# Half of the second load moved to ScalarE's ring, beside the first load

## The chip, the cores and the metric

One core of a Trainium2 chip. The metric is the device time of one execution in microseconds (us). Runs of one kernel mostly agree within 0.3%.

## The reference

A rotary embedding in float32: `x` of 16 x 512 x 1024 is cut into 16 heads of 64; each head's halves `x1`, `x2` are turned with `cos` and `sin` of 512 x 32.

```python
x1, x2 = x[..., :half_dim], x[..., half_dim:]
rotated = np.concatenate([x1 * cos - x2 * sin, x1 * sin + x2 * cos], axis=-1)
```

33.55 MB are read and as much is written.

## The kernel before

`x` is handled in 8 slabs of 2 batches: 128 partitions of 32 KB, 4.194 MB each. Five slabs fit at a time, so load 5 waits until store 0 has landed. Loads go through SyncE's ring (q1 in the profile), stores through ScalarE's ring (q10), the tables through GpSimd. Loads 1 to 4 are held until `cos` has landed.

```python
def load(s):
    slab[s] = slabs.tile([P, W], f32, tag="slab", name="slab")
    return nc.sync.dma_start(out=slab[s], in_=dram(x, s))

load(0)
# ... cos and sin are loaded through gpsimd
for s in range(1, slots):                 # slots = 5
    tc.add_manual_dep(load(s).ins, table[0].ins.name, ...)   # after cos
# ... tables, and passes: slabs 0, 6 and 7 in two halves, the others whole
cast(passes[0])                           # ScalarE: f32 slab -> bf16 xb
for i, (s, r, n) in enumerate(passes):
    if i + 1 < len(passes):
        cast(passes[i + 1])
    # ... VectorE: two products and a sum in bf16
    nc.scalar.copy(out=xs, in_=xu)        # ScalarE: bf16 -> f32, into the slab
    if r + n == rpp:
        nc.scalar.dma_start(out=dram(out_flat, s), in_=slab[s])
        if s + slots < nslabs:
            load(s + slots)
```

Of the kernel before, what the change touches and what calls it, by code (L numbers as in the profile page):

```python
# [2 lines left out]

# [4 lines left out]


@with_exitstack  # L10
def kernel(
    ctx: ExitStack,
    tc: tile.TileContext,
    x: bass.AP,
    cos: bass.AP,
    sin: bass.AP,
    num_heads: int,
    out: bass.AP,
):
    nc = tc.nc  # L20
    P = nc.NUM_PARTITIONS

    batch, seq, dim = x.shape
    nh = num_heads
    hd = dim // nh
    half = hd // 2
    bf16 = mybir.dt.bfloat16
    f32 = mybir.dt.float32

    nb = 2  # L30
    slots = 5
    nslabs = batch // nb
    rpp = nb * seq // P
    W = rpp * dim
    SP = seq // rpp
    TW = rpp * half

    out_flat = out.rearrange("b s h d -> b s (h d)")

    singles = ctx.enter_context(tc.tile_pool(name="singles", bufs=1))  # L40
    slabs = ctx.enter_context(tc.tile_pool(name="slabs", bufs=slots))
    xpool = ctx.enter_context(tc.tile_pool(name="xpool", bufs=2))
    psum = ctx.enter_context(tc.tile_pool(
        name="psum", bufs=1, space=bass.MemoryType.PSUM))


    def dram(t, s, a=0, n=W):
        return bass.AP(tensor=t.tensor, offset=t.offset + s * nb * seq * dim + a,
                       ap=[[W, P], [1, n]])


    def view(t, offset, *dims):
        return dataclasses.replace(t, offset=t.offset + offset,
                                   ap=[t.ap[0], *[list(d) for d in dims]])


    slab = {}


    def load(s):  # L60
        slab[s] = slabs.tile([P, W], f32, tag="slab", name="slab")
        return nc.sync.dma_start(out=slab[s], in_=dram(x, s))  # L62


    load(0)


    TR = seq // P
    G = rpp // TR
    table = {}  # L70
    raw = singles.tile([P, 2 * TR * half], f32, tag="raw")
    for i, src in enumerate((cos, sin)):
        table[i] = nc.gpsimd.dma_start(out=view(raw, i * TR * half, (1, TR * half)), in_=bass.AP(  # L73
            tensor=src.tensor, offset=src.offset,
            ap=[[TR * half, P], [1, TR * half]]))



    for s in range(1, slots):
        tc.add_manual_dep(  # L80
            load(s).ins, table[0].ins.name,
            mybir.DependencyInfo(mybir.DependencyClass.Sync,
                                 mybir.DependencyReason.DATA),
            reason="issue")



    pick = singles.tile([P, 2 * G * P], bf16, tag="pick")
    nc.gpsimd.memset(pick, 0.0)  # L89
    for g in range(2 * G):  # L90
        part = view(pick, g * P, (SP, P // SP), (1, SP))
        nc.gpsimd.affine_select(  # L92
            out=part, in_=part, compare_op=mybir.AluOpType.not_equal,
            fill=1.0 if g < G else -1.0, base=-(g % G),
            pattern=[[0, P // SP], [-G, SP]], channel_multiplier=1)

    tab1 = singles.tile([P, 2 * TR * half], bf16, tag="tab1")
    nc.gpsimd.tensor_copy(out=tab1, in_=raw)  # L98

    acc = psum.tile([P, 2 * rpp * hd], f32, tag="acc")  # L100
    for i in range(2):
        for h in range(2):
            for g in range(G):
                nc.tensor.matmul(  # L104
                    view(acc, (i * rpp + g * TR) * hd + h * half, (hd, TR), (1, half)),
                    view(pick, (i * h * G + g) * P, (1, P)),
                    view(tab1, i * TR * half, (half, TR), (1, half)),
                    start=True, stop=True)
    tab = singles.tile([P, 2 * rpp * hd], bf16, tag="tab")
    nc.vector.tensor_copy(out=tab, in_=acc)  # L110

    xb = {}


    def cast(u):
        s, r, n = u
        if r == 0:
            xb[s] = xpool.tile([P, W], bf16, tag="xb", name="xb")
        nc.scalar.copy(out=view(xb[s], r * dim, (1, n * dim)),  # L119
                       in_=view(slab[s], r * dim, (1, n * dim)))  # L120




    passes = []
    for s in range(nslabs):
        n = rpp if 1 <= s < nslabs - 2 else rpp // 2
        passes += [(s, r, n) for r in range(0, rpp, n)]


    cast(passes[0])
# [3 lines that stand above are left out]
        xs = view(slab[s], r * dim, (1, n * dim))  # L135
        xu = view(xb[s], r * dim, (1, n * dim))

        t2 = view(slab[s].bitcast(bf16), 2 * r * dim, (1, n * dim))
        for t, a in ((t2, rpp * hd), (xu, 0)):
            nc.vector.tensor_mul(  # L140
                out=t, in0=xu,
                in1=view(tab, a + r * hd, (hd, n), (0, nh), (1, hd)))
        nc.vector.tensor_add(  # L143
            out=xu, in0=xu, in1=view(t2, half, (hd, n * nh), (-half, 2), (1, half)))

        nc.scalar.copy(out=xs, in_=xu)  # L146
# [6 lines that stand above are left out]
# [1 line left out]
_INS = ['x', 'cos', 'sin', 'num_heads']  # L154
_OUTS = [((16, 512, 16, 64), 'float32')]

_NUMBERS = {'num_heads': 16}


# [26 lines left out]
```

## Time and profile before

| | before |
|---|---|
| median, 3 runs | 162.07 us (161.98 to 162.12) |
| VectorE, ScalarE busy | 68%, 71% |
| DMA rate over the span | 419 GB/s |
| slab 0 / slab 1 landed | 13.3 / 23.0 us |
| first store issued | 37.11 us |
| load 5 issued | 61.59 us |
| last store issued; until it landed | 145.28 us; 14.2 us |

The lines behind this stand in the prediction. They are read in this order: who is full, at what rate, where one stage hands over to the next, and how long the last transfer waits in its queue.

### The profile page before, as it was taken

To read this page: it belongs to the slowest core of one execution; us is meant where nothing else is said; L and a number is where in the kernel's file an instruction comes from. 1 tells how busy PE (TensorE), PEld (TensorE's weight loads), DVE (VectorE), ACT (ScalarE), POOL (GpSimd) and SP (SyncE) were. 2 spreads that over 40 slices of the span, in tenths; PEclk is the share of its full clock that TensorE was granted. 3 is DMA by queue.
4 is the path that set the end of the run, shared out by engine and by line. 5 is a ranking of instruction groups with operands and counts; after the bars stand their busy time and mean duration, and the time that the engine had idled before them with its cause. 6 is when DMAs were issued, how large, how long until landed. Compare 5 with 4: busy or idle time off the path is not lost.

```text
span 160.4 us, 169 instructions
## 1 busy us (share of the span) xinstructions
PE 1.0 (1%) x8; PEld 0.8 (1%) x8; DVE 108.5 (68%) x34; ACT 113.5 (71%) x23; POOL 3.4 (2%) x12
## 2 busy tenths in 40 slices
PE   0011000000000000000000000000000000000000
PEld 0010000000000000000000000000000000000000
DVE  0003799999989979997996099939749599930000
ACT  3006939998998999899907997099995999462000
POOL 7000000000000000000000000000000000000000
DMA  7999999999999999999999999999999999999995
GB/s 245 425 409 409 474 425 400 466 441 392 384 400 400 507 400 400 466 441 392 441 474 392 433 482 392 425 482 400 400 507 400 400 474 433 392 449 466 392 433 221
DMA packets 2368, 67.24 MB, mean 419 GB/s; under 512 B 288, under 2 KB 288, under 8 KB 320
## 3 DMA queue, kind: packets, MB, share of 16 engines
q1 hardware_dynamic: 1152, 33.55, 49.5%
q10 hardware_dynamic: 1152, 33.55, 48.4%
q0 software_dynamic: 64, 0.13, 0.2%
HBM read 33.69 MB, written 33.55 MB: 419 GB/s over the span
## 4 chain that ended last, share of the span: by engine, by line
DMA 59%; ACT 17%; issue 9%; DVE 4%; SPq 0%; ACTq 0%; POOLq 0%
DMA slab<-in_x_dram 39%; DMA out_dram<-slab 15%; ACT slab L146 11%; ACT xb L119 6%; DMA raw<-in_cos_dram 4%; DVE xb L140 1%; DVE xb L143 1%; DVE slab L140 1%; SPq L62 0%; ACTq L146 0%; POOLq L167 0%
## 5 line engine op out<-in xcount | busy, mean ns | idle before, releaser
L119 ACT CAST xb<-slab 128x4096 bf16<-128x4096 f32 (+1 forms) x11 | 56.6, 5155 | 27.5 <-DMA slab<-in_x_dram 26.2
L146 ACT CAST slab<-xb 128x4096 f32<-128x4096 bf16 (+1 forms) x11 | 56.6, 5153 | 3.5 <-DVE xb L143 3.5
L140 DVE TENSOR_TENSOR slab<-xb,tab 128x4096 bf16<-128x4096 bf16 (+1 forms) x11 | 35.9, 3260 | 19.9 <-ACT xb L119 19.8
L140 DVE TENSOR_TENSOR xb<-xb,tab 128x4096 bf16<-128x4096 bf16 (+1 forms) x11 | 35.9, 3261 | 0.3
L143 DVE TENSOR_TENSOR xb<-xb,slab 128x4096 bf16<-128x4096 bf16 (+1 forms) x11 | 35.9, 3261 | 0.3
L110 DVE CAST tab<-acc 128x1024 bf16<-128x1024 f32 x1 | 1.2, 1225 | 12.5 <-PE acc L104 12.5
L119 ACT ACT_TABLE_LOAD x1 | 1.3, 1283 | 0.7 <-PEq L167 0.7
L104 PE MATMUL acc<-tab,pick 128*128 128x128 bf16 x8 | 1.0, 305 | 11.5 <-POOL tab L98 11.5
L92 POOL TENSOR_SCALAR_AFFINE_SELECT pick<-pick 128x128 bf16<-128x128 bf16 x4 | 1.0, 288 | 0.1
L104 PEld LDWEIGHTS <-pick 128*128 128x128 bf16 x8 | 0.8, 136 | 11.4 <-issue 8.0
L73 POOL DMA_DIRECT2D raw<-in_cos_dram x1 | 0.7, 674 | 0.8 <-POOLq L167 0.8
L89 POOL MEMSET pick<- 128x512 bf16 x1 | 0.5, 543 | 0.0
L98 POOL CAST tab<-raw 128x256 bf16<-128x256 f32 x1 | 0.4, 396 | 6.9 <-DMA raw<-in_sin_dram 6.9
L73 POOL DMA_DIRECT2D raw<-in_sin_dram x1 | 0.5, 534 | 0.0
L167 POOL MEMSET const-float32-0.0<- 128x1 f32 x1 | 0.1, 99 | 0.2 <-issue 0.2
L167 POOL MEMSET const-bfloat16-1.0<- 128x1 bf16 x1 | 0.1, 102 | 0.0
L167 POOL MEMSET const-uint8-127<- 128x1 uint8 x1 | 0.1, 102 | 0.0
L167 POOL MEMSET const-float32-1.0<- 128x1 f32 x1 | 0.1, 99 | 0.0
## 6 DMA issues: line engine op xcount, KB each, us to landing
slab<-in_x_dram SPq DMA_DIRECT2D x8, 4096.0 KB, 24.5
out_dram<-slab ACTq DMA_DIRECT2D x8, 4096.0 KB, 26.6
raw<-in_cos_dram POOLq DMA_DIRECT2D x1, 64.0 KB, 7.0
raw<-in_sin_dram POOLq DMA_DIRECT2D x1, 64.0 KB, 9.0
```

Of the source, the lines that this page charges most:

```text
L73: table[i] = nc.gpsimd.dma_start(out=view(raw, i * TR * half, (1, TR * half)), in_=bass.AP(tensor=src.tensor, offset=src.offset, ap=[[TR * ...
L89: nc.gpsimd.memset(pick, 0.0)
L92: nc.gpsimd.affine_select(out=part, in_=part, compare_op=mybir.AluOpType.not_equal, fill=1.0 if g < G else -1.0, base=-(g % G), pattern=[[ ...
L98: nc.gpsimd.tensor_copy(out=tab1, in_=raw)
L104: nc.tensor.matmul(view(acc, (i * rpp + g * TR) * hd + h * half, (hd, TR), (1, half)), view(pick, (i * h * G + g) * P, (1, P)), view(tab1, ...
L110: nc.vector.tensor_copy(out=tab, in_=acc)
L119: nc.scalar.copy(out=view(xb[s], r * dim, (1, n * dim)), in_=view(slab[s], r * dim, (1, n * dim)))
L140: nc.vector.tensor_mul(out=t, in0=xu, in1=view(tab, a + r * hd, (hd, n), (0, nh), (1, hd)))
L143: nc.vector.tensor_add(out=xu, in0=xu, in1=view(t2, half, (hd, n * nh), (-half, 2), (1, half)))
L146: nc.scalar.copy(out=xs, in_=xu)
L167: nc = _bacc.Bacc("TRN2", target_bir_lowering=False, num_devices=1)
```

## The change

The intent is to use ScalarE's ring, which has nothing to do for the first 37 us, for a part of slab 1.

```diff
+    early = W // 2
...
     def load(s):
+        if s == 1:
+            return nc.sync.dma_start(out=view(slab[s], early, (1, W - early)),
+                                     in_=dram(x, s, early, W - early))
         slab[s] = slabs.tile([P, W], f32, tag="slab", name="slab")
         return nc.sync.dma_start(out=slab[s], in_=dram(x, s))
     load(0)
+    slab[1] = slabs.tile([P, W], f32, tag="slab", name="slab")
+    nc.scalar.dma_start(out=view(slab[1], 0, (1, early)), in_=dram(x, 1, 0, early))
```

## The prediction

> **What bounds the kernel now.** I read the page's totals first, then the two rings' bytes, the chain of waits, and last each stretch in which one stage hands over to the next. The totals (share of the span; then the mean DMA rate):
>
> ```profile
> PE 1.0 (1%) x8; PEld 0.8 (1%) x8; DVE 108.5 (68%) x34; ACT 113.5 (71%) x23; POOL 3.4 (2%) x12
> DMA  7999999999999999999999999999999999999995
> DMA packets 2368, 67.24 MB, mean 419 GB/s; under 512 B 288, under 2 KB 288, under 8 KB 320
> q1 hardware_dynamic: 1152, 33.55, 49.5%
> q10 hardware_dynamic: 1152, 33.55, 48.4%
> ```
>
> The two compute engines are 68% and 71% busy; the DMA engines are at nine tenths or more in 38 of 40 slices, and the two rings (q1 is SyncE's, with the loads; q10 ScalarE's, with the stores) add up to 98% of the span. So the DMA engines are the bound, and only their first and last slices have idle time. The table by stretch says how fast they go when full (columns: stretch, its length, busy time of the five engines, clock, DMA share, GB/s):
>
> ```profile
> 2.00:4.00 2.00, 0.00 (x0) 0.10 (x1) 0.00 (x0) 0.02 (x1) 1.93 (x6) 1.00 0.83 328
> 4.00:13.00 9.00, 1.01 (x8) 0.74 (x7) 0.49 (x1) 0.00 (x0) 0.47 (x2) 1.00 1.00 430
> 13.00:37.00 24.00, 0.00 (x0) 0.00 (x0) 20.67 (x9) 21.06 (x5) 0.00 (x0) 1.00 1.00 429
> 66.00:122.00 56.00, 0.00 (x0) 0.00 (x0) 42.99 (x13) 45.29 (x8) 0.00 (x0) 1.00 1.00 431
> ```
>
> The decisive row is 4 to 13 us: there the SyncE ring holds slab 0 alone for half of the time and already moves 430 GB/s, as much as both rings together do at 66 to 122 us (431). One ring fills the engines. A slab is 4.194 MB, so it costs 4.194 MB / 431 GB/s = 9.73 us of all the engines, in whichever ring it is.
>
> The timeline and the list of issues give the hand-overs (start, length, instruction, idle time before it; in the issue row, size and us from issue to landing):
>
> ```profile
> 0.74 9.34 SPq L62 DMA_DIRECT2D slab<-in_x_dram  x5
> 13.33 7.11 ACT L119 CAST xb<-slab 128x4096 bf16<-128x4096 f32 x2 [11.31 <-DMA slab<-in_x_dram]
> 23.05 7.02 ACT L119 CAST xb<-slab 128x8192 bf16<-128x8192 f32 x1 [2.61 <-DMA slab<-in_x_dram]
> 29.98 7.11 ACT L146 CAST slab<-xb 128x4096 f32<-128x4096 bf16 x2
> 37.11 0.38 ACTq L148 DMA_DIRECT2D out_dram<-slab  x1
> ...
> 145.28 0.34 ACTq L148 DMA_DIRECT2D out_dram<-slab  x1
> ...
> out_dram<-slab ACTq DMA_DIRECT2D x1, 4096.0 KB, 14.2
> ```
>
> Slab 0 lands at 13.3 us, slab 1 at 23.0, the first store is issued at 37.1, and the last store is issued at 145.28 and needs 14.2 us, to 159.5, which is the end. The chain of waits names loads (39% of the span), stores (15%) and ScalarE's casts (17%), but it follows one dependency at a time; with engines that are full throughout, a shorter link in it gains nothing unless the end moves.
>
> **What the Trainium skill says.** "DMA: Bandwidth & Descriptors", section "Issuing engines are not separate DMA queues": transfers of all issuers run on the same 16 engines and interleave, and issuing from several saves only issue time. The trace agrees: 430 GB/s with one ring, 431 with two; an issue costs 0.34 to 0.47 us. The same page, "Queues, rings and completion order": each engine takes turns between the rings that have work, by packets. The trace agrees: between 45 and 51.5 us q1 moved 1.47 MB and q10 1.54 MB. The same page, "Where 436 GB/s comes from", puts the ceiling at 435 GB/s; the 431 here is 1% below it, so no higher rate is to be expected.
>
> **The change, part by part.** Removed: nothing; bytes stay 67.24 MB. Added: one issue on ScalarE at the start (about 0.4 us, while it waits 11.3 us for slab 0 anyway), 128 rows of 16 KB where 128 rows of 32 KB become 256 of 16 KB, and a second landing for slab 1's cast to wait for. None is on the path.
>
> Moved: 2.10 MB now compete with slab 0 from the first microsecond. Slab 0 has 4.19 MB in 32 KB rows, the half slab the same number of rows of 16 KB; taking turns, both end together after 6.29 MB. So **slab 0 lands later by 2.10 MB / 431 GB/s = 4.9 us**, at 13.3 + 4.9 = 18.2. Slab 1 is complete when the same 8.39 MB have moved as before: 23.0. The second half of slab 1 and slabs 2 to 4 still wait for cos to land, at 8.3 us before and perhaps 10 with three queues taking turns; the SyncE ring holds slab 0 until about 18, so nothing starves. The tables (sin landed at 11.0, product ready at 13.7) come some 3 us later, still before the first cast ends at 18.2 + 3.6 = 21.8.
>
> ScalarE, if the order of its work stays: the two half casts 18.2 to 25.3, slab 1's cast (7.0) to 32.3 without the wait of 2.61 us that it has now, the two copies (7.1) to 39.5. VectorE starts at 21.8 instead of 17.0, and its six operations of 2.29 us end at about 35.5, before the second copy needs them (35.9). So the first store goes out at about 39.6 instead of 37.1: 4.9 minus nearly all of the 2.6 of idle time.
>
> What does that do to the DMA engines? While store 0 is missing, loads 3 and 4 are in the ring, so the engines stay full and the loads get ahead by what the store loses. Store 0 lands when five loads and itself have moved, 25.3 MB; at the 429 mean of the early stretches and a start at 1.6 us that is 60.6 us plus a short receipt. It landed at 37.1 + 24.4 = 61.5 before, so it was already close to that; I put the delay at 0.5 to 1.5 us. Load 5 reuses store 0's slab, so it moves by this **1 us**. The SyncE ring runs dry earlier (load 4 ends near 59 to 60, not 63.4), but the ScalarE ring has the rest of store 0 and store 1, which is issued near 56, so the engines don't idle; stores get ahead instead. From load 5 on, SyncE's ring was never dry again (load 6 is issued at 79.7 and load 5 lands at 85.2), so load 7 moves by the same 1 us, from 123.9 to about 125.
>
> The end: load 7's landing plus 21.4 us of casts and products (145.28 - 123.93) issues the last store, now at about 146.3. The store needs 9.73 us of transfer, about 1 us to begin (load 0: issued at 0.74, first packets between 1.4 and 1.8) and about 0.3 to be confirmed: an estimate of 11 to 12 us, against the 14.2 that it took. So it now waits **2 to 3 us behind store 6**, and a delay of 1 us fits in there. Sum on the end: 0 us, with some tenths for the smaller packets. The first 4 us, where the engines are 60% and 83% busy, might gain some tenths from a second ring. I predict 162.2 us, against 162.07.
>
> **Rivals.** (1) *The start is limited by one ring, and two fill it sooner.* For: share 0.83 at 2 to 4 us. Against: 430 GB/s from 4 us on. At most the missing 0.17 x 2 us plus a part of the 0.8 us missing before 2 us: 161.2 to 161.7. (2) *The later slab 0 reaches the end.* The whole 4.9 us would show only if ScalarE or VectorE were the bound; both have idle time before slab 5 (5.05 and 5.65 us waiting for its load and cast), which takes it up. If my slack of 2 to 3 us is overstated, or load 5 moves by the full 2.5 us, the end moves by 1 to 2: 163 to 164. (3) *The build orders the engines' work anew.* In the source the first copy of slab 0 comes before slab 1's cast; in the trace it comes after. An added transfer could turn such an order, in either direction; at the end, where casts and copies of slabs 6 and 7 alternate, one half copy (3.6 us) on the wrong side costs 3.6 minus the slack, 0.6 to 1.6 us: 163 to 164. (4) *The rings don't take turns at once* and slab 0 goes first: then it lands at 13.3 as before and nothing changes: 162.1.
>
> **Range and chances.** The middle case and (4) lie at 162.1 to 162.3, the gain of (1) at 161.2 or more, the losses of (2) and (3) up to 164. The range is 161.2 to 163.8. A change of 2% is 3.2 us, to 158.8 or 165.3: the first would take more than the idle time at the start, the second would take two of the losses together. Faster 0.01, same 0.96, slower 0.03.
>
> **What would show it.** In the profile after: slab 0's landing at about 18 us and slab 1's near 23; ScalarE's wait before slab 1's cast gone; the first store issued near 39.6; load 5 issued near 62.5, not 61.6; the last store issued 1 us later, with an issue to landing of about 13 us, not 14.2; DMA rate still 419 GB/s. Slab 0 at 13.3 would show that the rings don't take turns there. The prediction is wrong if the last store finds its ring empty, which shows as DMA idle time just before the last 10 us, or if the stretch of 0 to 4 us moves over 0.5 MB more than before.

## More of the kernel before

The order in which each engine does its work is fixed by the build and isn't always that of the source.

A DMA share a little over 1 comes from counting a transfer where it starts.

## The result, and the profile after

The changed kernel took **162.25 us** (median of 4 runs, 161.94 to 162.29); before took 162.02 in the same rounds. The ratio is 1.0009, 95% interval 0.9992 to 1.0027: no difference. Ratios here are the mean time of one kernel's fast runs over that of the other's of the same rounds, so not quite the ratio of the medians. Executions over 1.5% slower than the fastest of the same kernel are left out of the means.

From the page and the timeline of the changed kernel (the DMA total; then start, length, instruction and idle time before it):

```profile
DMA packets 2512, 67.24 MB, mean 419 GB/s; under 512 B 304, under 2 KB 304, under 8 KB 336
...
0.73 0.40 ACTq L73 DMA_DIRECT2D slab<-in_x_dram  x1
0.74 0.37 SPq L68 DMA_DIRECT2D slab<-in_x_dram  x1
...
18.30 14.03 ACT L127 CAST xb<-slab 128x4096 bf16<-128x4096 f32 x3 [15.85 <-DMA slab<-in_x_dram]
...
30.88 2.28 DVE L148 TENSOR_TENSOR xb<-xb,tab 128x4096 bf16<-128x4096 bf16 x1
...
33.08 4.42 DVE L148 TENSOR_TENSOR slab<-xb,tab 128x8192 bf16<-128x8192 bf16 x1
37.41 2.28 DVE L151 TENSOR_TENSOR xb<-xb,slab 128x4096 bf16<-128x4096 bf16 x1
...
39.78 3.60 ACT L154 CAST slab<-xb 128x4096 f32<-128x4096 bf16 x1 [3.94 <-DVE xb L151]
43.42 0.34 ACTq L156 DMA_DIRECT2D out_dram<-slab  x1
...
62.57 35.41 SPq L68 DMA_DIRECT2D slab<-in_x_dram  x3
...
145.59 0.34 ACTq L156 DMA_DIRECT2D out_dram<-slab  x1
```

Same bytes, same rate. The first cast starts 5 us later, at 18.30, and the wait before slab 1's cast is gone (the three casts run as one block of 14.03 us). But a new wait stands before the second copy back: 3.94 us for VectorE, which in this build does slab 1's first product (33.08, 4.42 us long) before the last sum of slab 0 (37.41). So the first store goes out at 43.42, 6.3 us later than before. Load 5 is issued 1.0 us later, and the last store only 0.3 us.

The next table, by stretch, shows the first 23 us, before and then after (stretch, length, busy time of the five engines, clock, DMA share, GB/s):

```profile
0.00:4.00 4.00, 0.00 (x0) 0.10 (x1) 0.00 (x0) 1.28 (x1) 2.89 (x11) 1.00 0.72 246
4.00:13.00 9.00, 1.01 (x8) 0.74 (x7) 0.49 (x1) 0.00 (x0) 0.47 (x2) 1.00 1.00 430
13.00:23.00 10.00, 0.00 (x0) 0.00 (x0) 6.74 (x4) 7.11 (x2) 0.00 (x0) 1.00 0.97 419
```

```profile
0.00:4.00 4.00, 0.00 (x0) 0.10 (x1) 0.00 (x0) 1.28 (x1) 2.89 (x11) 1.00 0.60 184
4.00:13.00 9.00, 0.00 (x0) 0.00 (x0) 0.00 (x0) 0.00 (x0) 0.15 (x2) 1.00 1.00 430
13.00:23.00 10.00, 1.01 (x8) 0.74 (x7) 2.29 (x2) 4.70 (x2) 0.32 (x1) 1.00 1.04 444
```

Multiplied out, 9.04 MB were moved by 23 us before, and 9.05 MB after. The second ring added nothing at the start.

### The profile page after: what moved, and what is told of

Same layout as the page of the kernel before. It is cut to its first block, busy times and chain, and to the rows that moved or that the text cites. A ratio compares the mean times of both kernels' runs of the same rounds, so it can differ in the third digit from the quotient of the medians.

```text
span 160.5 us, 173 instructions
## 1 busy us (share of the span) xinstructions
PE 1.0 (1%) x8; PEld 0.8 (1%) x8; DVE 108.3 (67%) x34; ACT 113.5 (71%) x23; POOL 3.4 (2%) x12
## 4 chain that ended last, share of the span: by engine, by line
DMA 43%; ACT 30%; DVE 14%; issue 3%; ACTq 0%; SPq 0%
DMA slab<-in_x_dram 27%; DMA out_dram<-slab 16%; ACT slab L154 15%; ACT xb L127 14%; DVE slab L148 7%; DVE xb L148 4%; DVE xb L151 3%; ACTq L156 0%; ACTq L154 0%; SPq L68 0%
## 6 DMA issues: line engine op xcount, KB each, us to landing
slab<-in_x_dram SPq DMA_DIRECT2D x1, 2048.0 KB, 14.2
```

## The experiments

Twelve kernels ran, all with correct results. Each was timed in 5 rounds beside the kernel before, whose medians were 162.18 in the first four runs, 162.27 in the next four and 162.20 in the last four.

### The delay without the second ring

The kernel before, with one added cast that delays all compute by 4.9 us:

```diff
+    nc.scalar.copy(out=view(xb[0], 0, (1, 5700)), in_=view(slab[0], 0, (1, 5700)))
     cast(passes[0])
```

> The kernel before, with one added ScalarE cast of 5700 elements (about 4.9 us) ahead of the first cast; no load is moved. It delays the compute by what the change delays it, without a second ring at the start. Theory (the engines of the DMA are the bound, compute has slack): first product near 21.9 us as after the change, first store near 43.4, load 5 issued 62.0 to 62.7, last store within 0.7 us of 145.3, time 162.0 to 162.5. Rival (the start delay reaches the end and the change hid it by a gain of the second ring): 164 to 167 us.

162.02 us (161.91 to 162.12), ratio 0.9987 (0.9975 to 1.0000). From its timeline:

```profile
13.44 4.94 ACT L132 CAST xb<-slab 128x5700 bf16<-128x5700 f32 x1 [11.43 <-DMA slab<-in_x_dram]
43.54 0.37 ACTq L150 DMA_DIRECT2D out_dram<-slab  x1
...
145.50 0.34 ACTq L150 DMA_DIRECT2D out_dram<-slab  x1
```

The build chose the same order on VectorE as in the changed kernel, and the first and the last store fall where they fell there. So a delay of 5 us at the start costs nothing by itself, and the second ring hid nothing.

### The slack of the last store

An added ScalarE copy just ahead of the last store: 1690 elements in one kernel, 4096 and 1100 in the other.

```diff
         nc.scalar.copy(out=xs, in_=xu)
+        if s == nslabs - 1 and r + n == rpp:
+            nc.scalar.copy(...)           # repeats a part of the copy above
```

> The kernel before, with one added ScalarE copy of 1690 elements (about 1.5 us) just ahead of the last store. Theory (the last store waits 2 to 3 us behind store 6): last store issued near 146.8, from issue to landing 12.7 instead of 14.2, time unchanged, 162.0 to 162.2. Rival (no slack at the end): 163.5.

> The same with two added copies, 4096 and 1100 elements (about 4.6 us). Theory (slack 2 to 3 us): last store near 149.9, from issue to landing 11 to 12, time 163.6 to 164.7. Rival without slack: 166.6. Rival with a slack over 4.6 us: 162.1.

With 1.5 us: 162.27 us, ratio 1.0003 (0.9989 to 1.0016). With 4.5 us: 163.20 us, ratio 1.0060 (1.0045 to 1.0074). The last store of each, its issue in the timeline and its time to landing in the list of issues; first with 1.5, then with 4.5:

```profile
146.13 0.34 ACTq L150 DMA_DIRECT2D out_dram<-slab  x1
out_dram<-slab ACTq DMA_DIRECT2D x1, 4096.0 KB, 13.3
```

```profile
149.67 0.34 ACTq L151 DMA_DIRECT2D out_dram<-slab  x1
out_dram<-slab ACTq DMA_DIRECT2D x1, 4096.0 KB, 11.1
```

A store with no other ahead of it needs 11.1 us; before, it took 14.2. So 14.2 - 11.1 = 3.1 us of it were waiting behind store 6, and that is the slack. (149.67 - 145.28 = 4.4 us later, minus 3.1, is 1.3; 1.0 was measured.) The expected time with 4.5 us, 163.6 to 164.7, was too high, because I had put the slack at 2 to 3 us.

### The same bytes ahead, in one ring

The half of slab 1 is issued in SyncE's ring, ahead of slab 0; ScalarE's ring stays empty:

```diff
-    load(0)
-    nc.scalar.dma_start(out=view(slab[1], 0, (1, early)), in_=dram(x, 1, 0, early))
+    nc.sync.dma_start(out=view(slab[1], 0, (1, early)), in_=dram(x, 1, 0, early))
+    nc.sync.dma_start(out=slab[0], in_=dram(x, 0))
```

> The same bytes ahead of slab 0 without a second ring: the first half of slab 1 is issued in SyncE's ring ahead of slab 0. Theory (bytes count, not rings): slab 0 lands near 18.3, slab 1 near 23.1, first store near 43.5, load 5 near 62.5, time 161.9 to 162.4, as after the change. Rival (the second ring in itself does something, good or bad): over 0.5 us away from the change.

162.33 us, ratio 1.0030 (1.0000 to 1.0059). First cast at 18.20, first store at 43.32, last store at 145.74: the changed kernel's times, with one ring. Bytes count, not rings. Two of its six runs took 163.51 and 163.64; both are in the ratio, and neither was profiled.

### The second ring without more bytes ahead

Slab 0's halves in the two rings, slab 1 as before:

```diff
-    load(0)
+    nc.sync.dma_start(out=view(slab[0], 0, (1, early)), in_=dram(x, 0, 0, early))
+    nc.scalar.dma_start(out=view(slab[0], early, (1, W - early)), in_=dram(x, 0, early, W - early))
```

> The second ring without extra bytes: the first half of slab 0 through SyncE's ring, the second through ScalarE's, slab 1 as before. Rival 1 of the prediction (one ring fills slowly, two sooner): slab 0 lands at 12.8 or earlier, more than 0.98 MB moved by 4 us, and 0.5 us off the end, 161.6. Theory (one ring is enough; in the trace of the change two rings moved less, not more, by 4 us: 0.74 against 0.98 MB): slab 0 lands at 13.3 to 13.9, 0.7 to 0.8 MB by 4 us, time 162.0 to 162.4.

162.32 us, ratio 1.0004 (0.9990 to 1.0019); the first cast starts at 13.52, against 13.33. Two rings don't bring slab 0 sooner than one. Two of its six runs took 165.19 and 165.77; they are not in the ratio or in the comparison (the four fast ones took 162.25 to 162.34).

### The change doubled, and where it begins to cost

All of slab 1 in ScalarE's ring beside slab 0:

```diff
     load(0)
+    nc.scalar.dma_start(out=slab[1], in_=dram(x, 1))
-    for s in range(1, slots):
+    for s in range(2, slots):
```

> The change doubled: all of slab 1 goes through ScalarE's ring beside slab 0. Theory: both land together near 23 us (8.39 MB at 431 GB/s), slab 0 thus 9.7 us later than before; casts 23.0 to 30.2, slab 1's to 37.2, first store near 48, store 4 near 105, but the waits before slabs 6 and 7 (4.1 and 1.8 us after the change) take up what is left: last store 145.3 to 146.5, within the slack that the run with 4.5 us on the last store gave (149.67 issued, 11.1 us to landing, against 145.28 and 14.2: 3.1 us). Five loads are done near 52, the first store starts before that, so no idle time: 162.0 to 162.7. Rival (delays of slab 0 reach the end in proportion): two times what the change cost, and that was nothing, so this rival needs over 165.

**166.43 us**, ratio 1.0264 (1.0223 to 1.0304). Its six runs spread more than those of the other kernels, from 165.41 to 167.72, and the profiled one is the slowest of them. My expectation failed here, though I had the first casts right (22.98) and the first store as well (48.10). By stretch, the changed kernel:

```profile
54.00:61.00 7.00, 0.00 (x0) 0.00 (x0) 6.93 (x3) 6.59 (x2) 0.00 (x0) 1.00 1.04 449
61.00:66.00 5.00, 0.00 (x0) 0.00 (x0) 4.00 (x2) 5.00 (x2) 0.00 (x0) 1.00 0.97 419
66.00:70.00 4.00, 0.00 (x0) 0.00 (x0) 3.97 (x2) 4.00 (x1) 0.00 (x0) 1.00 0.91 393
```

The doubled kernel's first two stores in its timeline, and then its stretches:

```profile
48.10 0.34 ACTq L150 DMA_DIRECT2D out_dram<-slab  x1
62.45 0.37 ACTq L150 DMA_DIRECT2D out_dram<-slab  x1
```

```profile
61.00:66.00 5.00, 0.00 (x0) 0.00 (x0) 4.96 (x2) 4.56 (x2) 0.00 (x0) 1.00 0.52 118
66.00:70.00 4.00, 0.00 (x0) 0.00 (x0) 2.97 (x2) 4.00 (x2) 0.00 (x0) 1.00 1.10 475
...
88.00:92.00 4.00, 0.00 (x0) 0.00 (x0) 3.97 (x2) 3.59 (x2) 0.00 (x0) 1.00 1.03 360
...
96.00:100.00 4.00, 0.00 (x0) 0.00 (x0) 2.99 (x2) 4.00 (x2) 0.00 (x0) 1.00 1.20 418
```

Five loads were done and store 0 had ended by 62 us; store 1 is only issued at 62.45, and load 5, which waits for store 0, at 62.48. Both rings were dry. From 61 to 70 us this kernel moved 0.118 x 5 + 0.475 x 4 = 2.49 MB, the changed one 3.67: 1.18 MB less, 2.7 us at 433 GB/s. By the shares, the engines stood idle for 9 - 5 x 0.52 - 4 x 1.10 = 2.0 us there, in the changed kernel for 0.5; so 1.5 of the 2.7 us are idle time, and the other 1.2 are transfers that took longer. I had checked that store 0 comes before the loads run out, and not that store 1 comes before store 0 runs out.

The other two rows show a second kind of loss: the engines are busy (1.03 and 1.20) but slower than a full share moves. I take 433 GB/s at a share of 1.00 as full speed, which the kernel before held from 82 to 122 us. Then the lost time is length x (share - rate / 433): 4 x (1.03 - 0.83) = 0.8 us and 4 x (1.20 - 0.97) = 0.9 us. With the 2.7 that makes 4.4. The profiled run was 5.5 us longer than the profiled run before (spans of 165.9 and 160.4 us), so about 1 us is not in this sum; against the median, 4.2, it would look complete by chance.

As a check, the same kernel with VectorE told to finish slab 0 first, so that both stores come sooner:

```diff
             mul = nc.vector.tensor_mul(...)
+            if s == 1 and a > 0:          # slab 1's first product
+                tc.add_manual_dep(mul.ins, summed.ins.name, ... NoSync ...)
         summed = nc.vector.tensor_add(...)
```

> The doubled change (whole slab 1 in ScalarE's ring, 166.43 us) with VectorE's order of before. There store 1 was issued at 62.45, after store 0 had moved its last bytes near 62.1, and load 5 at 62.48: both rings were dry, and 1.2 MB (2.8 us) were lost between 62 and 68. Theory: in this order the first store goes out near 44 and store 1 near 60.5, before the ring is dry, so this loss is gone: 162.2 to 164. Rival (slab 0's delay itself costs the 4 us): 166.

163.45 us, ratio 1.0075 (1.0063 to 1.0087); store 0 at 44.03, store 1 at 60.48. Slab 0 is as late as in the 166.43 run, and 3 of the 4 us are gone. So slab 0's delay by itself didn't cost them: they went with the dry stretch, its idle time and the slow transfers beside it. What remains is of the second kind:

```profile
62.00:74.00 12.00, 0.00 (x0) 0.00 (x0) 10.67 (x4) 12.00 (x2) 0.00 (x0) 1.00 0.99 401
74.00:82.00 8.00, 0.00 (x0) 0.00 (x0) 7.22 (x2) 7.59 (x2) 0.00 (x0) 1.00 1.01 393
```

12 x (0.99 - 0.93) + 8 x (1.01 - 0.91) = 1.5 us, against 1.25 measured.

### A larger delay of compute

The kernel before, with slab 0's copy back done once more (7.0 us of ScalarE):

```diff
+        if s == 0 and r + n == rpp:
+            nc.scalar.copy(out=slab[s], in_=xb[s])
```

(An ordering edge keeps slab 2's cast behind the first store.)

> The kernel before, with slab 0's copy back done a second time (7.0 us of ScalarE); in the build the first store then comes after slab 1's copy too, so it goes out near 51 us, 14 us later than before. Theory: five loads are done near 52, so the engines idle for at most 1 to 2 us; ScalarE's and VectorE's waits before slabs 5, 6 and 7 take up most of the shift, the last store goes out 2 to 5 us later, against a slack of 2 to 3; time 162.5 to 165. Rival (compute has no slack): 14 us of delay, about 176. Rival (nothing before 50 us matters at all): 162.0.

164.01 us, ratio 1.0123 (1.0102 to 1.0144). I had misread the built order: the first store went out at 44.35, 7 us later, and it is store 2 that came 13 us later (78.67 against 65.85). The last store was issued at 149.23, 0.8 us past the 148.4 that the slack of the kernel before allows, and a stretch of slow transfers was there again, 12 x (1.01 - 0.94) = 0.8 us:

```profile
110.00:122.00 12.00, 0.00 (x0) 0.00 (x0) 10.58 (x4) 9.53 (x3) 0.00 (x0) 1.00 1.01 407
```

The two don't add up: slow transfers hold up store 6 too, and with it the moment up to which the last store may come. It took 11.8 us to land, so it still waited 0.7 us of the 3.1. The pages' shares of the span give 1.2 us more of busy DMA engines than before and 0.3 more of idle ones; these 1.5 us are the difference of the two profiled spans, 161.9 and 160.4 us. So 13 us of delay in the middle mostly vanish, as the theory has it.

### The order on VectorE, and the moment of the first store

The changed kernel with VectorE's order of before (the ordering edge shown above), so that the first store comes where the prediction had put it:

> The changed kernel with VectorE's order of before: the sum of slab 0's second half ahead of slab 1's first product (in the changed build this product of 4.4 us came first). Theory: ScalarE's wait of 3.9 us before the second copy goes, first store at 39.5 as the prediction had it, not 43.4; stores 1 to 4 some 2 to 4 us sooner than after the change, load 5 at 62 to 62.6, and no effect on the end: 162.0 to 162.4. Rival (the order cost something that the second ring gave back): 161.5 or less.

The first store came at 39.17, as predicted, and the kernel became **slower**: 164.04 us, ratio 1.0114 (1.0095 to 1.0134). Three more kernels followed: this one with 0.6 and with 1.2 us of added copy ahead of the first store, and the kernel before with 2.1 us there:

```diff
+        if s == 0 and r + n == rpp:
+            nc.scalar.copy(...)           # 600, 1320 and 2400 elements
```

> The changed kernel with VectorE's order of before (it took 164.04 us), and one added ScalarE copy of 600 elements, about 0.6 us, ahead of the first store, which then goes out at 39.8 instead of 39.2. In the 164.04 run the DMA engines fell 0.3 MB behind between 74 and 82 us, without running dry, and load 5 landed 0.6 us later than after the change though it was issued 0.3 us later. Theory A (such a stall hangs on how loads and stores fall against each other, thus on the store's moment to within a transfer row of 1.2 us): the time moves by 0.5 us or more in one of this run and the next, towards 162.3. Theory B (VectorE's order itself costs 1.8 us): 164.0 in both.

> The same with 1320 elements, about 1.2 us: first store near 40.4. Theory A: 162.2 to 164, unlike the run with 0.6 us or unlike 164.04; theory B: 164.0.

> The kernel before with 2400 elements, about 2.1 us, ahead of the first store, which then goes out at 39.3, where the 164.04 run had it; no load is moved and VectorE's order is that of before. Theory (slack at the end, ScalarE's waits take up 2 us): 162.0 to 162.4. If the moment of the first store alone makes the stall: 163.5 to 164.5.

| kernel | first store at | median us | ratio (95%) |
|---|---|---|---|
| before | 37.1 | 162.2 | 1 |
| changed, VectorE as before | 39.2 | 164.04 | 1.0114 (1.0095 to 1.0134) |
| before + 2.1 us | 39.5 | 163.42 | 1.0082 (1.0068 to 1.0096) |
| changed, VectorE as before, + 0.6 us | 39.9 | 163.61 | 1.0096 (1.0069 to 1.0122) |
| changed, VectorE as before, + 1.2 us | 40.5 | 163.54 | 1.0082 (1.0069 to 1.0095) |
| changed | 43.4 | 162.25 | 1.0009 (0.9992 to 1.0027) |
| before + 4.9 us at the first cast | 43.5 | 162.02 | 0.9987 (0.9975 to 1.0000) |

The stretch of 74 to 82 us of four of these: before, changed, changed with VectorE as before, before + 2.1 us:

```profile
74.00:82.00 8.00, 0.00 (x0) 0.00 (x0) 7.97 (x2) 6.17 (x1) 0.00 (x0) 1.00 1.02 442
```

```profile
74.00:82.00 8.00, 0.00 (x0) 0.00 (x0) 6.96 (x3) 8.00 (x2) 0.00 (x0) 1.00 1.01 434
```

```profile
74.00:82.00 8.00, 0.00 (x0) 0.00 (x0) 6.96 (x3) 8.00 (x2) 0.00 (x0) 1.00 1.03 401
```

```profile
74.00:82.00 8.00, 0.00 (x0) 0.00 (x0) 6.96 (x3) 8.00 (x2) 0.00 (x0) 1.00 1.04 414
```

By the formula above nothing is lost in the first two and 0.8 and 0.7 us in the last two (0.7 and 1.0 us in the runs with 0.6 and 1.2). VectorE and ScalarE do as much there in the fast changed kernel as in the slow ones, so it isn't their work.

The kept traces say where the time goes. From 76 to 77 us SyncE's ring starts 16 load rows of 32 KB (0.52 MB) in each of the four slow kernels of the table and in the changed one. Its share there is 1.81 to 2.00 in the slow ones and 1.21 in the changed one: a row took about 1.8 to 2.0 us instead of 1.2. ScalarE's ring moves nothing (0.00 MB) meanwhile; in the slow kernels it has just ended store 1. Nor is the loss peculiar to them: when the first store begins, every kernel has it once (0.5 to 1.0 us by the formula). The kernel before has a share of 1.01 and 399 GB/s from 37 to 48 us, 11 x (1.01 - 0.92) = 1.0 us. The slow ones have it twice.

What follows: VectorE's order by itself isn't the cause, since before has it and is fast, and moving a load isn't either, since before + 2.1 us moves none and is slow. In the runs of this table the cost went with a first store between 39.2 and 40.5 us; but the doubled change with VectorE as before has the same loss at 74 to 82 us with a first store at 44.03, so that moment alone doesn't decide it. My sharper theory, that a shift within one transfer row of 1.2 us would undo it, isn't borne out: the two shifted runs came 0.4 and 0.5 us nearer to before, which just reaches the mark of 0.5 us that I had set, and not to it. Theory B, 164.0 in both, isn't either. The rest of their 1.2 to 1.8 us beyond the 0.7 to 1.0 of the formula is idle time (0.4 to 1.0 us more than before, by the shares of the span on their pages) at the very end, where the 16 engines no longer finish together: in the kernel of 164.04, two rows of 32 KB still start from 159 to 160 us (66 GB/s), and in the kernel before none after 158. Why the rows at 76 us take longer in these kernels stays open.

## Why the prediction was right or wrong, point by point

- **The bound, and the total.** Right: 162.25 against 162.2. The DMA engines stay full, and in these two kernels and the one-ring run neither the ring nor the order of the first loads changes their rate: 419 GB/s over the span before and after.
- **Slab 0 5 us later.** Right: 0.74 + 17.5 to landing = 18.2. Slab 1's second half, issued at 8.94, landed 14.2 us later, at 23.1. The rings took turns; rival 4 fell. The run with one ring shows that only the bytes ahead matter.
- **The first store at 39.6.** Wrong: 43.42. The failed step is "if the order of its work stays" carried over to VectorE: "its six operations of 2.29 us end at about 35.5". The build put slab 1's product of 4.42 us between them. It is rival 3, at the start instead of the end.
- **Load 5 near 62.5.** Right: 62.57, although store 0, for which it waits, went out 3.8 us later than predicted. That is because the estimate counted bytes (five loads and one store in all), and not the store's moment.
- **Last store near 146.3, 13 us to landing.** It was 145.59 and 13.8. The step "so load 7 moves by the same 1 us" failed: loads 6 and 7 were issued 1.4 and 1.3 us earlier than before (78.28 and 97.66 against 79.70 and 99.00), and slab 7's cast began at 124.27 instead of 123.96.
- **Slack of 2 to 3 us.** A little small: 3.1 us, as the run with 4.5 us showed.
- **Rival 1, a faster start.** Wrong: 9.05 against 9.04 MB by 23 us, and 162.32 us with slab 0 in both rings.
- **What the prediction lacked.** It took it for harmless when the first store goes out. With the store at 39.2, where the prediction wanted it, the same kernel takes 164.04, just outside the stated range. The total was right in part by luck: the step that failed spared the kernel this loss. And it didn't say how far the argument carries: at twice the dose both rings run dry, and the cost is some 4 us in all.

## What to carry to other kernels

When one ring already fills the DMA engines, a second ring only decides whose bytes come first, so ask what waits for the bytes that now come later. A delay was nearly free here as long as some ring had work at every moment and the slack of 3.1 us at the end lasted; with a ring dry at the wrong moment it was not. Check this for each hand-over (loads into first store, first store into second, last store behind its forerunner) and not for the first alone. Full rings were still no guarantee: the four kernels with a first store between 39.2 and 40.5 us lost 1.2 to 1.8 us without running dry. A build may reorder other engines when a load moves, so compare the order before trusting a timeline carried over from the old kernel.

## What the Trainium skill lacked or had wrong

- "DMA: Bandwidth & Descriptors", section "Issuing engines are not separate DMA queues", was right here: one ring 430 GB/s, two 431.
- The same page, "Specifications", gives a first-byte latency of about 0.6 us for SyncE's and ScalarE's transfers. With the other ring busy it was far longer: store 0 of the kernel before was issued at 37.11, and ScalarE's ring first moves data after 40.5, over 3 us later. Bytes by ring from 39 to 40.5 us, and then from 40.5 to 41.5:

```profile
q1 hardware_dynamic: 20, 0.66, 130.7%
...
q1 hardware_dynamic: 6, 0.20, 78.3%
q10 hardware_dynamic: 5, 0.16, 37.9%
```

- No page that I read has the loss of rate that came about the moment when a store begins to move beside queued loads: 373 to 414 GB/s at 74 to 82 us in the five kernels with this loss there, where before and changed have 442 and 434, and some 0.7 to 1.0 us each time; in four of them load rows took 1.8 to 2.0 us instead of 1.2. On what it depends was not found.
